# HGRN states loaded into idle split-weight buffers, prompt-state stores behind the weights, no chain offsets

## Chip, cores, metric

The kernel runs on one core of a Trainium2 chip. The metric is the device time of one execution in microseconds (us); lower is better. Of the kernel before there are three timed runs, with a median of 1349.09 us (1347.33 to 1349.79), and one profiled execution.

## What is computed

One inference step of a two-layer decoder trunk for a prompt of 256 tokens and, beside it, 8 sequences of 4 new tokens each ("sample") that carry state. All inputs are float32. For each layer:

```python
x = layer_norm(ALPHA * x + 0.5 * swiglu(x, ffn1_w_in, ffn1_w_out))
z = x @ mix_w_in                       # 1024 -> 1024 (RWKV) + 2048 (HGRN) + 512 (gMLP)
o_rw, s_rw, sh_rw = rwkv7_mix(z_rw, rw_shift0, rw_S0, ...)    # 4 heads x 64
o_hg, s_hg = hgrn2_mix(z_hg, hg_S0, lb, norm_g)               # 4 heads x 128
o_cm, v_cm = chunk_mlp_mix(z_cm, ...)
x = layer_norm(ALPHA * x + concat[o_rw, o_hg, o_cm] @ mix_w_out)
x = layer_norm(ALPHA * x + 0.5 * swiglu(x, ffn2_w_in, ffn2_w_out))
```

For the sample sequences HGRN starts from a carried state `state_hgrn` of 8 x 4 x 128 x 128 for each layer (2 MB): its output needs q times that state, and the new state is written out. For the prompt the state begins at zero. Outputs are the activations and, for each layer, the RWKV and HGRN end states of prompt and sample, the shift rows, and the normalised gMLP v rows of the sample (`cm_v_sample`).

## The kernel before

All 288 tokens lie along the free dimension, features along the partitions. Weights stream from HBM in blocks: `prep` (L338) loads one block of up to 4 x 128 rows and 256 columns (512 KB) into one of 3 buffers with the tag `raw`. For both feed-forward layers and the RWKV columns of the mixer (`rw_z`, L768) the block is then split into a high part (ScalarE, tag `wh`, 3 buffers) and a low part (VectorE, tag `wl`, 3 buffers), and each product takes three matmuls. For the HGRN and gMLP columns of `mix_w_in` (10 units of `hg_units`, L1325) and for `mix_w_out` the block is used as it is (pool "raw"), so `wh` and `wl` hold nothing between the end of `rw_z` and the first block of the second feed-forward. A `wh` or `wl` buffer is 4 KB in each partition, as is a state tile `s0` of [128, 8, 128] floats.

The mixer is written as 14 chains of small steps (`CHAINS`, L1790), generators that `mix` (L1708) walks round robin in `go`; after each step, `fill` (L435) emits one or more pieces of the ten dense units. So trace order alternates chains and dense work. A scheduler then orders each engine's instructions by priority, which is the trace position; `prio` (L83) moves the position of a chain, a step (in groups of four for a dense unit) or a chain of one layer ("@0") up by the number in `PR` (L1794), or down where it is negative. Engines run their instructions in that compiled order; a transfer issued by SyncE (SP) waits in SP's order for its buffer or its data.

The chains that matter here: `prompt` (`rw_prompt`, L952) and `post` for RWKV; `scan` (`hg_scan`, L1381), `hmix` (`hg_mix`, L1462) for the HGRN prompt; `hsam` (`hg_sample`, L1512) for the HGRN sample output, `hst` (`hg_states`, L1562) for its new states; `cm` (`cm_mix`, L1638). In `hsam`, V and K are transposed on TensorE (`hTs`, `h`) and split (`hk`); GpSimd builds masked queries `hqm`; the four states `s0` (program name `hs`) are loaded at L1544 into tiles of the tag `m4` (19 buffers shared with most mixer tiles); 64 matmuls `hp` read `hs` and `hqm`; then squares `hsqs`, a reduce and a reciprocal `hrm`, and the scaled output `hos`. `hst` updates `hs` in place and stores it (L1592). `hmix` forms `hO` for two halves of the prompt, normalises them through `hsq`, `hrm`, `hon`, transposes them back (`hot`), and stores its end state `hSP` at L1502. `rw_prompt` stores `rwSo` at L1150. `cm_mix` stores `cvn` at L1666. When the mixer outputs `x` are ready, `post` (L525) runs `mix_w_out` over them: first the k-blocks 0, 1, 6, 7 (RWKV and gMLP), then 2 to 5 (HGRN).

Of the kernel before, what the change touches and what calls it, by code (L numbers as in the profile page):

```python
# [8 lines left out]
F32 = mybir.dt.float32  # L9
# [11 lines left out]
NS = 32  # L21
# [17 lines left out]
class Trunk:  # L39
# [298 lines left out]
    def prep(self, spec):  # L338

        name, l, ks, n0, pool = spec  # L340
        nk = len(ks)
        nc = self.nc
        raw = self.wp.tile([128, 4, 256], F32, tag="raw", name=f"raw{nc.next_id()}", bufs=B["raw"])
        runs = [i for i in range(nk + 1) if i in (0, nk) or ks[i] != ks[i - 1] + 1]
        for a, b in zip(runs, runs[1:]):
            src = self.I[name][l][ks[a] * 128:(ks[b - 1] + 1) * 128, n0:n0 + 256]
            nc.sync.dma_start(raw[:, a:b], src.rearrange("(c p) n -> p c n", p=128))
        if pool == "raw":
            return raw
        hi = self.wp.tile([128, 4, 256], F32R, tag="wh", name=f"wh{nc.next_id()}", bufs=B["wh"])  # L350
        lo = self.wp.tile([128, 4, 256], F32R, tag="wl", name=f"wl{nc.next_id()}", bufs=B["wl"])
        with self.prio("prep"):
            self.act(hi[:, :nk], raw[:, :nk])
            self.sub(lo[:, :nk], raw[:, :nk], hi[:, :nk].bitcast(F32), nc.gpsimd if pool else None)
        return hi, lo
# [596 lines left out]
    def rw_prompt(self, l, KR, bh, kh, V, eP, em):  # L952

        nc, O = self.nc, self.O
# [43 lines left out]
        for qi, src in ((0, bh), (2, kh)):  # L998
# [3 lines left out]
            for h in range(2):  # L1002
                pv = ps[h].rearrange("p (j c q n) -> p j c q n", j=2, c=2, q=2)
                for k, mk in ((0, self.mst64), (1, self.min64)):
                    v = AT[qi + k].rearrange("p (j g) n -> p j g n", j=2)[:, :, 2 * h:2 * h + 2]
# [6 lines left out]
            if qi == 0:  # L1012
# [4 lines left out]
                for h in range(2):  # L1017
                    p = ps[h][:, 0:256].rearrange("p (j c n) -> p j c n", j=2, c=2)
                    v = D.rearrange("p (j g) n -> p j g n", j=2)[:, :, 2 * h:2 * h + 2]
# [8 lines left out]
        for j in range(2):  # L1028
            js = slice(j * 128, (j + 1) * 128)
            for i, src in enumerate((V, bh, kh, KR[:, :, 0])):  # L1030
                p = self.ps(f"pT{l}{j}{i}")
# [11 lines left out]
        for b in (2, 4, 8, 16, 32):  # L1043
            Ab = self.ep.tile([128, 8, 64], F32, tag="Ab", name=f"Ab{l}{b}", bufs=B["Ab"])
            self.mul(Ab, AT[0], bc(self.nmt64[b], 8), self.eng("Ab"))
            p = self.ps(f"pX{l}{b}")
            self.mm(p, self.idb, self.id8.rearrange("p g n -> p (g n)"), True, False)
            p = g8(p)
# [96 lines left out]
        p = self.ps(f"pSo{l}")  # L1145
        for c in range(2):
            self.tr(p[0:64, c * 128:(c + 1) * 128], S[:, c, 3])
        so = self.ep.tile([64, 256], F32, tag="rwSo", name=f"rwSo{l}", bufs=1)
        nc.vector.tensor_copy(so, p[0:64, 0:256])
        nc.sync.dma_start(O["rwkv_state_prompt"][l, 0].rearrange("g v k -> v g k"),  # L1150
                          so.rearrange("p (g k) -> p g k", g=4))

    def rw_load(self, l):
        nc, I = self.nc, self.I
# [307 lines left out]
    def hg_mix(self, l):  # L1462
        nc, O = self.nc, self.O
        Q, P, K, V = [self.hg(n) for n in "QPKV"]
        AT = self.hs[0]
        VT = self.m4([128, 2, 4, 128], f"hVT{l}")
        KT = self.m4([128, 2, 4, 128], f"hKT{l}")
        for i, (src, dst) in enumerate(((V, VT), (K, KT))):
            for j in range(2):
                p = self.ps(f"hT{l}{j}{i}")  # L1470
                for h in range(4):
                    self.tr(p[:, h * 128:(h + 1) * 128], self.hpr(src)[:, h, 128 * j:128 * j + 128])
                self.act(dst[:, j].rearrange("p h n -> p (h n)"), p)
                yield
        SP = self.a2(f"hSP{l}").rearrange("p c n -> p (c n)")[:, 0:512].rearrange("p (h n) -> p h n", h=4)
        on = self.m4([128, 2, 4, 128], f"hon{l}")
        self.hon = on
        for j in range(2):
            js = slice(128 * j, 128 * j + 128)
            p = self.ps(f"hO{l}{j}").rearrange("p (h n) -> p h n", h=4)  # L1480
            for h in range(4):
                self.mm(p[:, h], AT[:, 4 * j + h], VT[:, j, h], h == 0, j == 0 and h == 3)
            if j == 1:
                for h in range(4):
                    self.mm(p[:, h], self.hpr(Q)[:, h, js], SP[:, h], False, h == 3)

            sq = self.a2(f"hsq{l}{j}").rearrange("p c n -> p (c n)")[:, 0:512].rearrange("p (h n) -> p h n", h=4)
            self.act(sq, p, AF.Square)
            r = self.hrms(f"{l}{j}", sq, 4)
            self.mul(on[:, j], p, r.unsqueeze(2).to_broadcast([128, 4, 128]))  # L1490
            self.done.add(f"hm{j}{l}")
            yield
            p = self.ps(f"hS{l}{j}").rearrange("p (h n) -> p h n", h=4)
            for h in range(4):
                self.mm(p[:, h], KT[:, j, h], VT[:, j, h])
            if j == 0:
                self.act(SP, p)
            else:
                for h in range(4):
                    self.stt(SP[:, h], SP[:, h], P[:, 256 * h + 255:256 * h + 256], p[:, h], ALU.mult, ALU.add)  # L1500
            yield
        nc.sync.dma_start(O["hgrn_state_prompt"][l, 0].rearrange("h k v -> k h v"), SP)  # L1502

    def hrms(self, nm, sq, n):
        nc = self.nc
        r = self.ep.tile([128, 4], F32, tag="hrm", name=f"hrm{nm}", bufs=2)[:, 0:n]
        nc.vector.tensor_reduce(r, sq, axis=AX.X, op=ALU.add)
        self.act(r, r, AF.Sqrt, bias=self.eps[:, 2:3], scale=1.0 / 128)
        nc.vector.reciprocal(r, r)
        return r  # L1510

    def hg_sample(self, l):  # L1512
        nc, I, O = self.nc, self.I, self.O
        gp = nc.gpsimd
        SB = 4 * T
        Q, P, K, V = [self.hg(n) for n in "QPKV"]
        AS = self.hs[1]


        vs = self.ep.tile([128, 128], F32, tag="hvs", name=f"hvs{l}", bufs=1)  # L1520
        p = self.ps(f"hTs{l}")
        self.tr(p[:, 0:128], V[:, SB:])
        self.act(vs, p[:, 0:128])
        k3 = self.m4([128, 2, 4, 128], f"hk3{l}", F32R)
        for i, src in ((0, K), (1, V)):
            r3 = self.a2(f"r3{l}{i}").rearrange("p c n -> p (c n)")[:, 0:384].rearrange("p (h r t) -> p h r t", h=4, r=3)
            gp.tensor_copy(r3, self.hsm(src).unsqueeze(2).to_broadcast([128, 4, 3, 32]))
            p = self.ps(f"h3{l}{i}")
            for h in range(4):
                self.tr(p[0:96, h * 128:(h + 1) * 128], r3[:, h].rearrange("p r t -> p (r t)"))  # L1530
            pv = p.rearrange("p (h n) -> p h n", h=4)
            self.act(k3[0:96, i], pv[0:96])
            lo = slice(32, 64) if i == 0 else slice(64, 96)
            self.sub(k3[lo, i], pv[lo], k3[lo, i].bitcast(F32))
            yield

        qm = self.m4([128, 4, 8, 32], f"hqm{l}")
        for h in range(4):
            self.mul(qm[:, h], self.hsm(Q)[:, h].unsqueeze(1).to_broadcast([128, 8, 32]), self.tb, gp)
        S0 = []  # L1540
        for h in range(4):
            s0 = self.m4([128, 8, 128], f"hs0{l}{h}")
            S0.append(s0)
            nc.sync.dma_start(s0, I["state_hgrn"][l, :, h].rearrange("b k v -> k b v"))  # L1544

        p = self.ps(f"hp{l}")[:, 0:128]
        for b in range(8):
            for h in range(4):
                self.mm(p[32 * h:32 * h + 32], qm[:, h, b], S0[h][:, b], b == 0, False)
            if b % 2:  # L1550
                yield
        self.mm(p, AS, vs, False, True)
        sq = self.e(f"hsqs{l}")[:, 0:128]
        self.act(sq, p, AF.Square)
        r = self.hrms(f"{l}s", sq, 1)
        os = self.ep.tile([128, 128], F32, tag="hvs", name=f"hos{l}", bufs=1)
        self.act(os, p, scale=r)
        self.hos = os
        yield
        self.hst = S0, k3  # L1560

# [76 lines left out]
    def cm_mix(self, l, cw, m):  # L1638
# [6 lines left out]
        for j, (o, n) in enumerate(((0, 128), (128, 128), (T, NS))):  # L1645
            p = self.ps(f"cT{l}{j}")
            for c in range(2):
# [15 lines left out]
        v = vn.rearrange("p (j h) d -> p j (h d)", j=3)  # L1663
        self.mul(v, v, gb[:, 0].unsqueeze(1).to_broadcast([128, 3, 256]), gp)
        self.add(v, v, gb[:, 1].unsqueeze(1).to_broadcast([128, 3, 256]), gp)
        nc.sync.dma_start(O["cm_v_sample"][l].rearrange("b t d -> (b t) d"),  # L1666
                          vn[0:NS, 8:12].rearrange("p h d -> p (h d)"))
        yield
        M = self.a2(f"cM{l}")
        for j in range(2):  # L1670
# [37 lines left out]
    def mix(self, l, q, x, st):  # L1708
# [30 lines left out]
        def chain(name, g, *names):  # L1739

            while not all(f"{n}{l}" in self.done for n in names):
                yield False
            yield from g()
            self.done.add(f"{name}{l}")
# [15 lines left out]
        def post(f):  # L1760
# [2 lines left out]
            return f(l, q, rw["o"], *self.rwv[6:], lambda: mt(0))  # L1763

        self.rw_load(l)
        ch = {
            "pre": (pre,),
            "prompt": (lambda: self.rw_prompt(l, *rw["v"]), "pre"),
# [14 lines left out]
        m = m[0]  # L1783
        r = self.post(("mix_w_out", l), m, KC, 1.0, q["ln"][1], SHIFT[1], GROUPS[E["mo"]])
        go(*[(chain(n, *ch[n]), f, n) for n, f in CHAINS if n in LATE])
        return r


# [2 lines left out]
          ('cm', 1), ('post', 1), ('houts', 1), ('hout', 1), ('hou0', 3), ('scan', 1)]  # L1791
LATE = ()

PR = {'prep': 250, 'posts': 450, 'hou0': -50, 'scan': 400, 'hsam': -150, 'post': -400, 'scan.4': 20,  # L1794
      'cm.1': 200, 'q1.0': -7, 'hmix': 20, 'hst.6': 100, 'sample.0': -20, 'hmix.7': -20, 'posts@1': -400,
      'sample.2': 50, 'houts@0': 200, 'prompt.19': -7, 'houts': 50, 'scan@0': 400, 'houts.0': -50, 'prompt.22': 200,
      'o1': 7}

E = {'gn': 'v', 'gm': 'v', 'LN': 1, 'th': 't', 'xl': 'p', 'R1': 'p', 'mo': 'r', 'om': '', 'vb': (0, 2), 'hs': (0, 1,
     2, 3), 'Ab': 'p', 'RV': 'v', 'LL': 'v', 'S': 'p', 'P': 'p', 'KS': 'v'}  # L1800
# [43 lines left out]
```

## Time and profile before

| | before |
|---|---|
| median of 3 runs | 1349.09 us |
| the profiled execution: its own time | 1349.48 us |
| its span, first to last instruction | 1347.8 us |
| mean granted TensorE clock | 0.992 |
| TensorE matmul busy | 1315.4 us (98%) |
| VectorE, ScalarE, GpSimd busy | 65%, 44%, 16% |
| DMA, mean over the span | 144 GB/s |

Busy time is counted from the profiler's records; a matmul's end is modelled. TensorE is the engine to watch; idle time of another engine matters only where TensorE waits for it. The two mixers stand at about 250 to 465 us and 909 to 1121 us. Times in all rows are microseconds from the start of the span. "PEclk" is the granted clock as a share of full speed; "DMA share" is the mean busy share of the core's 16 DMA engines.

### The profile page before, as it was taken

How to read it: one execution, taken by the hardware profiler on the slowest of the kernel's cores; microseconds unless marked ns; L12 is line 12 of the kernel's file. 1: busy time of each engine (PE TensorE's matmuls, PEld its weight loads, DVE VectorE, ACT ScalarE, POOL GpSimd, SP SyncE). 2: the span in 40 equal slices, each digit the busy share in tenths (PEclk: the TensorE clock that was granted, in tenths of full speed). 3: DMA queues.
4: the chain of work that ended last, by engine and by line, in shares of the span. 5: the costliest groups of instructions: out<-in, count | busy, mean ns of one | idle time of the engine just before them, and what ended most of it. 6: DMA issues, size and time to landing. Idle time of an engine off the chain costs nothing.

```text
span 1347.8 us, 26357 instructions
## 1 busy us (share of the span) xinstructions
PE 1315.4 (98%) x10714; PEld 1213.6 (90%) x10714; DVE 869.9 (65%) x1670; ACT 599.2 (44%) x974; POOL 221.5 (16%) x361
## 2 busy tenths in 40 slices
PE   8999999999998999999999999999999999999998
PEld 6999999867767799999999999997777769999998
DVE  4555447865435697774698775597744359877643
ACT  5454435743143364443465444367322516544433
POOL 9200001335334100000100000022453221000002
PEclk9999999999998999999999999999999999999998
DMA  5655455431235555554555554553122455555551
GB/s 179 191 159 171 156 166 165 127 95 49 75 110 164 161 172 157 171 157 157 162 167 163 166 159 159 168 157 109 59 75 68 138 163 180 161 168 162 179 162 50
DMA packets 208151, 194.03 MB, mean 144 GB/s; under 512 B 15911, under 2 KB 206363, under 8 KB 208030
## 3 DMA queue, kind: packets, MB, share of 16 engines
q1 hardware_dynamic: 207326, 190.91, 46.0%
q8 instruction: 84, 1.38, 0.4%
q0 software_dynamic: 608, 1.31, 0.4%
q14 instruction: 37, 0.30, 0.1%
q10 hardware_dynamic: 96, 0.13, 0.0%
HBM read 185.10 MB, written 7.22 MB: 143 GB/s over the span
## 4 chain that ended last, share of the span: by engine, by line
PE 90%; DVE 5%; DMA 2%; issue 1%; ACT 1%; POOL 1%; SPq 0%; DVEq 0%; ACTq 0%
PE d L97 78%; PE hA L97 1%; DMA raw<-in_ffn_w_in 1%; PE pX L97 1%; DMA raw<-in_mix_w_out 1%; PE pE L97 1%; PE pD L97 1%; DVE ax L65 1%; PE lnd L97 1%; DVE wl L65 1%; DVE zs L77 1%; PE hp L97 0%; PE yp L97 0%; ACT wh L62 0%; PE pO L97 0%
## 5 line engine op out<-in xcount | busy, mean ns | idle before, releaser
L97 PE MATMUL d<-x,wh 128*128 128x290 f32 (+1 forms) x3072 | 623.0, 298 | 0.0
L97 PEld LDWEIGHTS d<-x,wh 128*128 128x128 f32 x3072 | 498.3, 190 | 1.5
L65 DVE TENSOR_TENSOR wl<-raw,wh 128x1024 fp32r<-128x1024 f32 (+1 forms) x288 | 346.0, 1202 | 230.2 <-ACT wh L62 229.2
L62 ACT ACTIVATE wh<-raw 128x1024 fp32r<-128x1024 f32 (+1 forms) x288 | 298.2, 1035 | 431.9 <-PE d L97 267.5
L97 PE MATMUL d<-x,wl 128*128 128x290 f32 (+1 forms) x1536 | 457.6, 298 | 2.2 <-DVE wl L65 2.2
L97 PEld LDWEIGHTS d<-x,wl 128*128 128x128 f32 x1536 | 291.2, 190 | 2.6 <-ACT x L62 2.3
L97 PE MATMUL d<-h,wh 128*128 128x288 f32 x1408 | 282.1, 296 | 0.0
L97 PEld LDWEIGHTS d<-h,wh 128*128 128x128 f32 x1408 | 226.3, 188 | 0.2
L97 PE MATMUL d<-h,wl 128*128 128x288 f32 x704 | 207.9, 295 | 0.0
L97 PE MATMUL d<-ax,raw 128*128 128x288 f32 x640 | 173.9, 414 | 0.0
L65 POOL TENSOR_TENSOR lnv<-lnq,lnq 128x288 f32<-128x288 f32 x6 | 7.6, 1273 | 840.0 <-ACT lnq L62 840.0
L97 PEld LDWEIGHTS d<-ax,raw 128*128 128x128 f32 x640 | 115.2, 190 | 30.3 <-issue 2.0
L97 PEld LDWEIGHTS d<-h,wl 128*128 128x128 f32 x704 | 132.4, 188 | 0.2
L97 PE MATMUL d<-x,raw 128*128 128x288 f32 x256 | 66.8, 409 | 2.3 <-DMA raw<-in_mix_w_out 1.6
L97 PEld LDWEIGHTS d<-x,raw 128*128 128x128 f32 x256 | 47.8, 190 | 17.0 <-DVE lns L65 1.8
L77 DVE SCALAR_TENSOR_TENSOR ax<-d,ax 128x288 f32<-128x288 f32 x48 | 21.6, 454 | 49.1 <-PE d L97 49.1
L62 ACT ACT_TABLE_LOAD x39 | 50.0, 1283 | 5.0 <-DVE yg L77 3.5
L62 ACT ACTIVATE sg<-yg,ccg 128x288 f32<-128x288 f32 x66 | 34.7, 528 | 35.3 <-DVE yg L77 35.2
L62 ACT ACTIVATE h<-sg 128x288 fp32r<-128x288 f32 x88 | 37.7, 435 | 21.7 <-DVE sg L65 20.9
L65 DVE TENSOR_TENSOR h<-sg,h 128x288 fp32r<-128x288 f32 x88 | 39.5, 454 | 5.6 <-ACT h L62 5.6
L77 DVE SCALAR_TENSOR_TENSOR yu<-nu,ccu,yu 128x288 f32<-128x288 f32 x66 | 34.0, 515 | 0.8
L77 DVE SCALAR_TENSOR_TENSOR yg<-nu,ccg,yg 128x288 f32<-128x288 f32 x66 | 33.9, 516 | 0.8
(477 smaller groups left out, 1291.1 us busy)
## 6 DMA issues: line engine op xcount, KB each, us to landing
raw<-in_ffn_w_in SPq DMA_DIRECT2D x176, 512.0 KB
raw<-in_ffn_w_out SPq DMA_DIRECT2D x80, 512.0 KB
raw<-in_mix_w_in SPq DMA_DIRECT2D x56, 512.0 KB
raw<-in_mix_w_out SPq DMA_DIRECT2D x12, 512.0 KB
raw<-in_ffn_w_out SPq DMA_DIRECT2D x16, 256.0 KB
hs<-in_state_hgrn SPq DMA_DIRECT2D x8, 512.0 KB
out_hgrn_state_sample<-hs SPq DMA_DIRECT2D x8, 512.0 KB
raw<-in_mix_w_out SPq DMA_DIRECT2D x8, 256.0 KB
```

The costliest lines, as they stand in the source:

```text
L62: self.nc.scalar.activation(out, in_, func, **kw)
L65: (eng or self.nc.vector).tensor_tensor(out, a, b, op=op)
L77: self.nc.vector.scalar_tensor_tensor(out, a, s, b, op0=op0, op1=op1)
L97: self.nc.tensor.matmul(out, lhsT, rhs, start=start, stop=stop)
```

## The change

The four HGRN state tiles of a layer are no longer `m4` tiles loaded inside `hsam`. A new function `hg_load`, called by `mix` right after `rw_load`, takes two `wh` and two `wl` buffers for them and issues the four loads on SP, behind the last weight load traced so far (`issue_after` fixes the issue order on SP and adds no wait for that load); at that place in the trace it is the last block of `rw_z`. The prompt-state stores of `rw_prompt` and `hg_mix` are collected in a list and issued at the end of `mix`, behind the last load of `mix_w_out`. The store of `cm_v_sample` goes from SP's queue to GpSimd's. All entries of `PR` but `prep` are dropped. `prep` remembers its last load.

```diff
@@ prep
-            nc.sync.dma_start(raw[:, a:b], src.rearrange("(c p) n -> p c n", p=128))
+            self.lastraw = nc.sync.dma_start(raw[:, a:b], src.rearrange("(c p) n -> p c n", p=128))
@@ rw_prompt
-        nc.sync.dma_start(O["rwkv_state_prompt"][l, 0].rearrange("g v k -> v g k"),
-                          so.rearrange("p (g k) -> p g k", g=4))
+        self.late.append((O["rwkv_state_prompt"][l, 0].rearrange("g v k -> v g k"),
+                          so.rearrange("p (g k) -> p g k", g=4)))
@@ hg_mix
-        nc.sync.dma_start(O["hgrn_state_prompt"][l, 0].rearrange("h k v -> k h v"), SP)
+        self.late.append((O["hgrn_state_prompt"][l, 0].rearrange("h k v -> k h v"), SP))
@@ new
+    def hg_load(self, l):
+
+        self.hs0 = []
+        with self.tc.issue_after(self.lastraw.ins if hasattr(self.lastraw, "ins") else self.lastraw):
+            for h in range(4):
+                s0 = self.wp.tile([128, 8, 128], F32, tag=("wh", "wl")[h % 2], name=f"hs0{l}{h}", bufs=3)
+                self.nc.sync.dma_start(s0, self.I["state_hgrn"][l, :, h].rearrange("b k v -> k b v"))
+                self.hs0.append(s0)
@@ hg_sample
-        S0 = []
-        for h in range(4):
-            s0 = self.m4([128, 8, 128], f"hs0{l}{h}")
-            S0.append(s0)
-            nc.sync.dma_start(s0, I["state_hgrn"][l, :, h].rearrange("b k v -> k b v"))
+        S0 = self.hs0
@@ cm_mix
-        nc.sync.dma_start(O["cm_v_sample"][l].rearrange("b t d -> (b t) d"),
-                          vn[0:NS, 8:12].rearrange("p h d -> p (h d)"))
+        gp.dma_start(O["cm_v_sample"][l].rearrange("b t d -> (b t) d"),
+                     vn[0:NS, 8:12].rearrange("p h d -> p (h d)"))
@@ mix
         self.rw_load(l)
+        self.hg_load(l)
+        self.late = []
...
         r = self.post(("mix_w_out", l), m, KC, 1.0, q["ln"][1], SHIFT[1], GROUPS[E["mo"]])
         go(*[(chain(n, *ch[n]), f, n) for n, f in CHAINS if n in LATE])
+
+        with self.tc.issue_after(self.lastraw.ins if hasattr(self.lastraw, "ins") else self.lastraw):
+            for dst, src in self.late:
+                self.nc.sync.dma_start(dst, src)
@@ module
-PR = {'prep': 250, 'posts': 450, 'hou0': -50, 'scan': 400, 'hsam': -150, 'post': -400, 'scan.4': 20,
-      'cm.1': 200, 'q1.0': -7, 'hmix': 20, 'hst.6': 100, 'sample.0': -20, 'hmix.7': -20, 'posts@1': -400,
-      'sample.2': 50, 'houts@0': 200, 'prompt.19': -7, 'houts': 50, 'scan@0': 400, 'houts.0': -50, 'prompt.22': 200,
-      'o1': 7}
+PR = {'prep': 250}
```

## Rows read from the trace of the kernel before

**Rows 1.** The page: busy time, share of the span and instructions of each engine.

```profile
PE 1315.4 (98%) x10714; PEld 1213.6 (90%) x10714; DVE 869.9 (65%) x1670; ACT 599.2 (44%) x974; POOL 221.5 (16%) x361
```

**Rows 2.** Windows, first mixer's tail: length, busy (count) by engine, PEclk, DMA share, GB/s.

```profile
382.50:396.60 14.10, 14.10 (x60) 11.06 (x59) 3.80 (x7) 3.38 (x6) 4.83 (x5) 1.00 0.54 153
...
402.10:408.00 5.90, 0.02 (x1) 0.05 (x2) 4.98 (x11) 3.63 (x7) 4.09 (x8) 0.72 0.94 273
408.00:412.50 4.50, 4.50 (x25) 4.10 (x26) 0.00 (x0) 1.59 (x3) 0.00 (x0) 0.60 1.03 259
...
458.80:465.30 6.50, 6.50 (x32) 5.98 (x33) 5.06 (x9) 4.16 (x8) 0.54 (x1) 0.74 0.62 194
```

**Rows 3.** Windows, second mixer's tail: busy of PE, PEld, DVE, ACT, POOL; clock; DMA.

```profile
1060.70:1069.50 8.80, 5.91 (x61) 4.32 (x60) 5.94 (x16) 7.01 (x12) 6.03 (x5) 1.00 0.93 247
...
1082.80:1085.40 2.60, 0.06 (x1) 0.07 (x2) 1.82 (x5) 1.12 (x4) 2.60 (x2) 1.00 0.56 187
```

**Rows 4.** Waits of TensorE in both tails: total us, times, longest.

```profile
PE hp L97 <- DVE hgO L77: 5.9, 1, 5.9
...
PE d L97 <- DMA raw<-in_mix_w_out: 1.4, 1, 1.4
...
PE hot L101 <- DVE hon L65: 2.5, 1, 2.5
...
PE hT L101 <- DVE hk L65: 1.5, 1, 1.5
```

**Rows 5.** Timeline of SP, both tails: start, length of the issues, what, count.

```profile
402.23 5.70 SPq L1544 DMA_DIRECT2D hs<-in_state_hgrn  x4
...
428.35 5.96 SPq L1592 DMA_DIRECT2D out_hgrn_state_sample<-hs  x4
434.40 9.91 SPq L347 DMA_DIRECT2D raw<-in_mix_w_out  x4
...
1053.97 0.46 SPq L1544 DMA_DIRECT2D hs<-in_state_hgrn  x1
1059.74 0.61 SPq L1150 DMA_DIRECT2D out_rwkv_state_prompt<-rwSo  x1
```

**Rows 6.** Timeline of VectorE and GpSimd, first tail; the bracket is idle time before.

```profile
398.59 0.86 DVE L65 TENSOR_TENSOR cM<-cbs,cO 128x256 f32<-128x256 f32 x2 [12.04 <-PE cO L97]
...
402.12 2.53 POOL L65 TENSOR_TENSOR hqm<-hgQ,tb 128x256 f32<-128x256 f32 x4
```

**Rows 7.** Timeline of VectorE, second tail.

```profile
1083.13 0.28 DVE L1507 TENSOR_REDUCE hrm1s<-hsqs 128x1 f32<-128x128 f32 x1 [8.38 <-ACT hsqs L62]
```

**Rows 8.** Windows, start of the first mixer, columns as in rows 2.

```profile
249.90:255.40 5.50, 5.50 (x43) 5.50 (x42) 5.50 (x18) 3.97 (x8) 3.08 (x10) 1.00 0.67 170
255.40:262.50 7.10, 6.66 (x34) 5.25 (x34) 6.73 (x21) 5.82 (x11) 4.13 (x14) 1.00 0.23 57
```

**Rows 9.** Timelines of SP and TensorE, start of the first mixer.

```profile
261.46 0.33 SPq L809 DMA_DIRECT2D out_rwkv_shift_prompt<-sho  x1
...
262.55 0.53 SPq L347 DMA_DIRECT2D raw<-in_mix_w_in  x1
...
266.65 6.47 PE L97 MATMUL d<-ax,raw 128*128 128x288 f32 x26
```

**Rows 10.** Chain that ended last: a weight load's landing, and the split after it.

```profile
447.83 3.63 DMA raw<-in_ffn_w_in
451.48 1.06 ACT wh L62
```

**Rows 11.** Windows, the middle of each mixer, columns as in rows 2.

```profile
300.00:382.00 82.00, 81.48 (x1230) 62.73 (x1232) 39.59 (x79) 21.98 (x46) 34.10 (x32) 1.00 0.22 66
...
959.00:1041.00 82.00, 81.94 (x1249) 63.11 (x1247) 39.46 (x78) 22.21 (x47) 34.20 (x33) 1.00 0.23 66
```

**Rows 12.** SP's wait for the gMLP rows; a GpSimd-issued transfer's time on GpSimd.

```profile
SPq L1666 <- POOL cvn L65: 3.4, 1, 3.4
...
400.21 0.53 POOL L1632 DMA_DIRECT2D cbs<-in_cm_bs  x1 [12.50 <-DVE cM L65]
```

## The prediction

> **What bounds the kernel now.** I read the page first: TensorE is busy for 98% of the span [rows 1], so a change can win only what TensorE idles or loses to a low clock: 1347.8 - 1315.4 = 32.4 us of idleness. The windows say where. The middles of both mixers are full, 81.5 and 81.9 of 82 us [rows 11]; the tails are not. In the first tail TensorE does nothing for 5.9 us, then works 4.5 us at a granted 0.60 [rows 2]; in the second it is idle for 8.80 - 5.91 = 2.9 us and later for 2.60 - 0.06 = 2.5 us [rows 3]. The waits of TensorE name the instructions: `hp`, `hT` and `hot` [rows 4].
>
> Two things stand behind these waits. **The states come late.** In the first layer SP issues the four state loads only at 402.23 [rows 5], just when TensorE has run out of work. The window moves 5.9 us x 273 GB/s = 1.6 MB and the next one 4.5 x 259 = 1.2 MB [rows 2], together what the 2.1 MB of states, one weight block of 0.5 MB and a small store need. In the second layer the first load goes at 1053.97, then SP stands at the RWKV prompt-state store until 1059.74, with three loads behind it [rows 5]. **The other engines wait for TensorE's order.** From 382.5 to 396.6 TensorE runs almost only dense matmuls of `o1`, `o0`, while VectorE, ScalarE and GpSimd are busy 3.8, 3.4 and 4.8 of 14.1 us [rows 2]; VectorE idles 12.04 us until `cO`, and `hqm` begins at 402.12, after the dense work it could have run beside [rows 6]. `hsam` carries -150, so its transposes stand behind those dense pieces.
>
> **Early state loads.** Removed from the tails: 2 x 4 loads of 512 KB and what waits for them. In the first layer I count the whole hole, 5.9 us, and the low clock after it, 4.5 x (1 - 0.60) = 1.8 us [rows 2]. In the second layer 2.9 us: three of four loads land inside that window, which moves 247 GB/s at a DMA share of 0.93 [rows 3]; 1.5 us of it is put down to `hk` [rows 4], so it could also return nothing. The 2.5 us wait of `hot` follows from the same lateness: `hrm1s`, the sample's reduce, stands on VectorE ahead of the prompt's `hrm` and waits until 1083.13 for `hsqs`, made from the last `hp` [rows 7]. With states early, `hp` ends early and this wait goes; bounds 0 and 2.5. Sum: 5.9 + 1.8 + 2.9 + 2.5 = 13.1 us.
>
> **What the loads cost where they go.** They need two `wh` and two `wl` buffers, which come free as the last RWKV blocks are consumed, some 6 us before the dense units begin at about 256. From 249.90 to 255.40 the DMA engines are 0.67 busy, from 255.40 to 262.50 only 0.23 [rows 8]: free are 5.5 x 0.33 + 7.1 x 0.77 = 7.3 us. The loads need 2.1 MB / 273 GB/s = 7.7 us. SP stands still there anyway, for the shift-row store at 261.46 [rows 9]. So I count 0, because all but 0.4 us fits; the other bound is a weight load put behind all four, below. On the far side, the second feed-forward's first split is at 451.48 [rows 10], while the state stores are issued from 428.35 and SP has gone on at 434.40 [rows 5]: the buffers are wanted 17 us after SP has passed the stores, and one of three is free throughout. Cost 0; gone if `hst` slips by more than that. Four `m4` buffers come free in the tail; that can only advance allocations there, and I count nothing.
>
> **Stores moved.** The RWKV store (0.61 us of issue) and the HGRN one no longer stand ahead of state loads and stores; the second layer's block at 1059.74 is contained in the 2.9 us. They land in SP's queue beside the first feed-forward loads, 320 KB for each layer, 1.2 us at 273 GB/s. A weight load there takes 3.63 us to land and then feeds the first split [rows 10]; bounds 0 and 1.2 us a layer. I take 0, since SP waits for a buffer before those loads. They are moved past the last `mix_w_out` loads; the 1.4 us wait for one of them [rows 4], behind the sample-state stores [rows 5], stays or goes, bounds 0 and -1.4; I leave it. The gMLP store frees SP of a 3.4 us wait and costs GpSimd about one issue, 0.53 us by its nearest row [rows 12]; nobody reads its result and GpSimd idles in that window, so 0.
>
> **Offsets dropped.** No instruction is added or removed; orders change. Removing -150 lets `hTs`, `h`, `hqm` and the splits run under the 14.1 us of dense work [rows 2], which is what the first term needs to be won. Removing +400 (+800 in the first layer) of `scan` could slow it, but the layers, with 800 and 400, and 450 and 50 for `posts`, have almost the same counts and busy times in the middle [rows 11]: offsets of this size hardly decide there. Something new will be last, though: the `hot` and `hk` waits are the nearest sizes, 2.5 and 1.5 us [rows 4], mean 2.0, and I charge one in each layer; bounds 0 and 5.9, the longest tail wait. Given back: 4.0 us.
>
> **Sum.** 13.1 - 4.0 = 9.1 us. Against the profiled execution's own 1349.48 us that is 1340.4; it stands 0.4 us above the median, so I predict 1340.0. A measurement of this kernel tells 0.2%, 2.7 us, from no change.
>
> **Rival 1: the weights wait behind the states** (slower, 0.17). If the four loads get ahead of the dense units' weight load, issued at 262.55 and used by the matmuls at 266.65 [rows 9], they delay it. A landing takes 3.6 us [rows 10], so slack is 4.1 - 3.6 = 0.5 us; a full 7.7 us ahead of it costs 7.2 us a layer, 14.4 in all, less 9.1: 1354.4 us. It decides once more than some 0.4 + 0.5 = 0.9 us of state transfers are still to come at 262.5. Against: the 7.3 free us, and buffers that come free 6 us before. For: SP's order is fixed by estimated times, and a small slip there moves four loads. The Trainium skill, "DMA: Bandwidth & Descriptors", section "Queues, rings and completion order", says that SP's transfers share one set of rings whose descriptors are consumed in order; by that rule a load queued early is no free load, and this change would come out slower wherever a weight load stands behind it. Rows 5 agree so far: three state loads stood behind one store.
>
> **Rival 2: the hole was not the states'** (no change, 0.11). The profile names `hgO` on VectorE, not a load, as what ended the 5.9 us [rows 4]. If VectorE's chain sets it, early states win nothing in the first layer (7.7 us less), and 9.1 - 7.7 = 1.4 us stays: 1348. Against: `hp` reads `hs` and `hqm`, nothing that `hgO` writes, and the transfers fill that window.
>
> **Rival 3: partly** (faster, 0.12). The first layer's hole goes, the second's waits are those of `hk` and `hon` and stay: 7.7 - 4.0 = 3.7 us, 1345.7.
>
> **Rival 4: a later chain** (slower, 0.08). Without `scan`'s offset the HGRN prompt ends after the dense work; TensorE then waits twice a layer for what is now hidden. It decides when the chain slips by more than the 14.1 us of cover [rows 2]; at 5.9 us a layer and nothing won, 1349.5 + 11.8 = 1361.
>
> **The numbers.** My forecast has 0.52. Its own range is 1332 to 1345: all 13.1 us with nothing given back, with the 1.4 us and with the low clock of 458.80 to 465.30, 6.5 x 0.26 = 1.7 us [rows 2], gives 1333; 1345 is the edge to rival 3. Faster by over 0.2%: 0.52 + 0.12 = 0.64; within: 0.11; slower: 0.17 + 0.08 = 0.25. The range runs from 1332 to 1354, up to rival 1; above it are half of that and rival 4, below it little.
>
> **What would show it.** Right: no state load on SP in either tail, state loads between about 250 and 262; `hTs` and `hqm` before the last dense pieces of `o0`; no `hp` wait over 1 us; the clock at 1.00 through the first tail; full windows at the start of the mixers. Wrong: TensorE waiting for `raw` of `mix_w_in` near 262 (rival 1), an equal hole before `hp` under another name (rival 2), or VectorE's `hon` or `hSP` as last link of a longer tail (rival 4).

## The result and the profile after

The changed kernel takes 1331.28 us, the median of 4 runs (1329.77 to 1333.56), beside 1349.44 us of the kernel before. The ratio is 0.9869, 95% interval [0.985, 0.9888]: 18.2 us or 1.3% faster. The forecast had the direction, with 9.1 us half of the size; the result is 0.7 us below the low end of the range. The profiled execution after took 1330.73 us, with a span of 1329.0 us and a granted clock of 0.998.

The page's first part after, to be held against [rows 1]:

```profile
PE 1303.8 (98%) x10714; PEld 1203.5 (91%) x10714; DVE 860.6 (65%) x1670; ACT 598.5 (45%) x974; POOL 221.4 (17%) x363
```

The same 10714 matmuls. The span fell by 18.8 us. TensorE's idle time, span less busy, went from 32.4 to 25.2 us, only 7.2 us of that; the other 11.6 us left its busy time. But for 1.8 us of low clock, that was in no step of the prediction. To find the place, each mixer's tail is cut from the last `pO` of the RWKV prompt to the end of `lnva`, the layer norm behind `mix_w_out`. The same 64 dense matmuls of the HGRN units are left over at the start of it in both kernels. First the kernel before, then the one after, windows of the two tails (columns as in rows 2):

```profile
382.55:465.32 82.77, 72.88 (x412) 58.39 (x412) 44.66 (x90) 31.82 (x70) 26.66 (x26) 0.94 0.55 161
1041.17:1121.45 80.28, 72.70 (x412) 55.84 (x412) 41.78 (x90) 31.83 (x70) 23.44 (x19) 1.00 0.53 157
```

```profile
383.29:455.33 72.04, 69.27 (x411) 54.65 (x412) 41.81 (x90) 31.73 (x70) 27.26 (x27) 1.00 0.50 151
1032.19:1104.31 72.12, 69.28 (x411) 54.64 (x412) 41.81 (x90) 31.84 (x70) 23.98 (x20) 1.00 0.48 145
```

The tails are 10.7 and 8.2 us shorter, 18.9 us in all. Idle in them fell from 9.9 and 7.6 us to 2.8 each, 11.9 us together; busy time fell by 3.6 and 3.4 us. In the second tail the granted clock was 1.00 in both kernels, so those 3.4 us are not the clock's. Outside the tails three small differences cancel: the two heads of the mixers (from `z` to the last `pO`) grew by 0.6 and 1.1 us, the feed-forward layers between the mixers stayed within 0.1 us, and the stretch from the second tail to the end of the program is 1.7 us shorter. That last one is no work of the change: its same matmuls ran at another granted level. Windows of the last 5 us with dense work, before and after:

```profile
1335.00:1340.00 5.00, 5.00 (x29) 4.67 (x28) 1.11 (x6) 2.42 (x4) 0.00 (x0) 0.66 0.01 2
```

```profile
1316.20:1321.20 5.00, 5.00 (x40) 4.68 (x40) 1.20 (x6) 2.42 (x4) 0.00 (x0) 1.00 0.00 0
```

29 matmuls against 40 in 5 us. The changed kernel itself, profiled once more, ended at 0.66 with 28 matmuls in such a window. A difference of 1 to 2 us between two profiled executions is therefore not to be read as the change's.

Waits of TensorE in the first tail after, and below the dots in the second (total us, times, longest):

```profile
PE lnd L97 <- DVE ax L77: 1.8, 1, 1.8
PE d L97 <- DMA raw<-in_mix_w_out: 0.9, 1, 0.9
...
PE lnd L97 <- DVE ax L77: 1.7, 1, 1.7
PE d L97 <- DVE lns L65: 1.1, 1, 1.1
```

Against [rows 4], `hp`, `hot` and `hT` are gone and no wait of the HGRN chains has come in their place. `lnd` is the layer norm, which waited 1.8 us before as well.

Timeline of SP after, first mixer (start, length, what, count):

```profile
250.16 3.60 SPq L1518 DMA_DIRECT2D hs<-in_state_hgrn  x3
253.79 6.66 SPq L1160 DMA_DIRECT2D sn<-in_state_rwkv  x8
...
262.63 0.58 SPq L1518 DMA_DIRECT2D hs<-in_state_hgrn  x1
263.32 0.52 SPq L347 DMA_DIRECT2D raw<-in_mix_w_in  x1
...
395.70 19.88 SPq L347 DMA_DIRECT2D raw<-in_mix_w_out  x6
419.99 5.73 SPq L1597 DMA_DIRECT2D out_hgrn_state_sample<-hs  x4
425.82 9.85 SPq L347 DMA_DIRECT2D raw<-in_mix_w_out  x4
435.72 0.61 SPq L1796 DMA_DIRECT2D out_rwkv_state_prompt<-rwSo  x1
```

Against [rows 5, 9]: the states go at 250 to 262.6, the dense units' weight load moved only from 262.55 to 263.32, and `mix_w_out` starts at 395.70 (before: 390.54).

Timeline of TensorE after, first tail:

```profile
385.81 0.60 PE L101 MATMUL hT<-ident,hgV 128*128 128x128 f32 x4
386.25 1.14 PE L97 MATMUL d<-ax,raw 128*128 128x288 f32 x4
387.31 1.09 PE L97 MATMUL cO<-cwt,cvn 128*64 128x128 f32 x16
...
393.86 0.64 PE L97 MATMUL hp<-hs,hqm 128*32 128x128 f32 x16
394.43 1.24 PE L97 MATMUL d<-ax,raw 128*128 128x288 f32 x4
...
396.92 0.60 PE L101 MATMUL pgt<-ident,OM 128*128 128x128 f32 x4
```

Where before 58 dense matmuls stood in one block, they now stand in groups of 4 to 8, with every chain's matmuls between them. Timeline of TensorE before:

```profile
382.48 14.33 PE L97 MATMUL d<-ax,raw 128*128 128x288 f32 x58
```

`cO`, on which VectorE waited 12.04 us [rows 6], is done by 389.

### The profile page after: what moved, and what is told of

It reads as the page before. It is cut to its first block, busy times and chain, and to the rows that moved or that the text cites. A ratio compares the mean times of both kernels' runs of the same rounds, so it can differ in the third digit from the quotient of the medians.

```text
span 1329.0 us, 26345 instructions
## 1 busy us (share of the span) xinstructions
PE 1303.8 (98%) x10714; PEld 1203.5 (91%) x10714; DVE 860.6 (65%) x1670; ACT 598.5 (45%) x974; POOL 221.4 (17%) x363
## 4 chain that ended last, share of the span: by engine, by line
PE 89%; DVE 4%; DMA 2%; issue 2%; ACT 1%; POOL 1%; SPq 0%; POOLq 0%; ACTq 0%; DVEq 0%
PE d L97 79%; PE hA L97 1%; DMA raw<-in_ffn_w_in 1%; PE pX L97 1%; DMA cws<-in_cm_ws 1%; PE pE L97 1%; PE pD L97 1%; DVE wl L65 1%; PE lnd L97 0%; DVE DE L65 0%; PE hO L97 0%; ACT wh L62 0%; DMA raw<-in_mix_w_out 0%; PE hp L97 0%; DVE ax L65 0%
## 5 line engine op out<-in xcount | busy, mean ns | idle before, releaser
L97 PE MATMUL d<-ax,raw 128*128 128x288 f32 x640 | 182.1, 418 | 0.0
```

The source lines that it names most:

```text
L97: self.nc.tensor.matmul(out, lhsT, rhs, start=start, stop=stop)
```

## Experiments

Each ratio is to the kernel before, timed beside it, with its 95% interval.

### One part alone

**Early states.** Kernel after with the old `PR`, both prompt-state stores and the `cvn` store as before.

```diff
-PR = {'prep': 250}
+PR = {'prep': 250, 'posts': 450, ..., 'o1': 7}
-        self.late.append(...)
+        nc.sync.dma_start(...)
```

> Only the four early state loads of each layer into the idle wh and wl buffers; the old offsets, store places and the SP store of the gMLP rows stay. Theory A (the late states made the holes; the order of the rest matters little): the 5.9 us hole before hp, the low clock after it and the 2.5 us wait of hot go, 10 to 13 us less than before, about 1338. Theory B (TensorE's order made them: hsam's -150 keeps the transposes behind 14 us of dense work, and the matmuls stay in small pieces): hp still waits for hk or hqm, 3 to 7 us less than before, about 1344, and the tails still keep TensorE busy for about 72.7 us each.

1347.95 us, 0.9985 [0.9973, 0.9998]: about 2 us. The hole is gone, yet other waits stand there. Waits of TensorE, whole span:

```profile
PE pgt L101 <- DVE OM L65: 4.1, 2, 2.1
PE d L97 <- DVE x L65: 4.1, 2, 2.8
```

So the prediction's main term, as a term of the loads, falls.

**Offsets.** Kernel before with `PR = {'prep': 250}`, nothing else.

> Only the offsets dropped (all but prep); states still loaded inside hsam into m4 tiles, stores in their old places. Theory A: the loads still come late or stand ahead of weight loads, so at most 3 us less than before, or slower by up to 5 us: 1346 to 1354. Theory B: the interleaved order alone wins 8 us or more, below 1341, with TensorE busy for about 69.3 us in each tail.

1337.55 us, 0.9908 [0.9888, 0.9929]: some 12 us, two thirds of the gain, with the loads still inside `hsam`. They now stand on SP at 392.45 instead of 402.23 [rows 5]:

```profile
392.45 5.63 SPq L1544 DMA_DIRECT2D hs<-in_state_hgrn  x4
```

**Stores.** Kernel before with the late prompt-state stores and the `cvn` store on GpSimd.

> Only the two prompt-state stores of each layer queued behind the last mix_w_out load, and the gMLP rows stored from GpSimd's queue. Both theories: the RWKV store no longer stands ahead of three state loads in the second layer, so some of its 2.9 us goes, 0 to 3 us less than before, 1346 to 1349; the first layer's 5.9 us hole stays.

1347.12 us, 0.9982 [0.997, 0.9994]: some 2 us. The state loads go at 400.86, 1.4 us earlier, and TensorE's wait now carries their name:

```profile
PE hp L97 <- DMA hs<-in_state_hgrn: 5.2, 2, 4.6
```

`hp` starts there at 405.95, before VectorE ends `hgO` at 407.19. That answers rival 2: `hp` does not wait for `hgO`, and the 5.9 us ascribed to it [rows 4] are read as a wait for the states, too. The three parts alone sum to 12.4 + 2.0 + 2.4 = 16.8 of about 17.7 us by ratios; they hardly help each other.

### One part undone

**State loads back in `hsam`**, as `m4` tiles, the rest as after.

> The changed kernel with the state loads put back inside hsam and into m4 tiles; stores late and offsets dropped. Theory A: it loses most of the gain, 1342 to 1350, with a wait of TensorE for hp of 3 us or more in one tail at least. Theory B: it keeps most, below 1337.

1336.42 us, 0.99 [0.9882, 0.9919]. Timeline of SP:

```profile
377.20 12.65 SPq L347 DMA_DIRECT2D raw<-in_mix_w_in  x3
389.94 5.15 SPq L1553 DMA_DIRECT2D hs<-in_state_hgrn  x4
```

**Idle buffers, late load.** As after, but `hg_load` is called inside `hsam`.

```diff
-        self.hg_load(l)
...
+        self.hg_load(l)
         S0 = self.hs0
```

> The changed kernel with the state tiles in the idle wh and wl buffers but traced where hsam needs them, behind the last weight load traced by then. If the early time of the loads is worth the 5.1 us that putting the loads back cost, this kernel shows that loss too, about 1336, and hp waits for hs. If the four freed m4 buffers are worth it, it stays at the changed kernel's 1331.

1331.68 us, 0.9871 [0.9854, 0.9888], the changed kernel's time with loads 130 us later. SP:

```profile
376.55 5.40 SPq L347 DMA_DIRECT2D raw<-in_mix_w_in  x2
382.00 5.12 SPq L1518 DMA_DIRECT2D hs<-in_state_hgrn  x4
388.83 0.37 SPq L347 DMA_DIRECT2D raw<-in_mix_w_in  x1
```

Earliness is not what pays. The `wh` and `wl` buffers are empty when the loads' turn comes, and they are issued at 382.00, ahead of the last `mix_w_in` block. The `m4` tiles are not: SP waits 1.6 us for ScalarE (`qs`) and 0.3 us for VectorE (`gst`) before these loads, which read only from HBM, and at 389.94 they stand behind that block. That the buffers alone set this place is not shown, since `hg_load` also brings `issue_after`. These 8 us are worth some 4 us (1336.42 against 1331.68, intervals that overlap by 0.0006).

**Fewer `m4` buffers.** As after, with 15 instead of 19, the four that the states left.

> The changed kernel with 15 m4 buffers instead of 19, so the four that the states left are taken away. If those buffers are what the state part wins (5.1 us lost with the loads put back): about 5 us slower than the changed kernel, 1336. If not: 1331, and the loss came from the loads' place in SP's queue.

1333.84 us, 0.9882 [0.9868, 0.9895]. **The kernel after once more**, beside it:

> The changed kernel itself, once more, as the yardstick of this group: 18 us less than before, a ratio of 0.987.

1332.29 us, 0.9873 [0.9859, 0.9886]. The 1.5 us between them lie within the intervals: the four freed buffers have no effect that could be told. **Stores as before**, the rest as after:

> The changed kernel with the three stores back in their old places and queues. The RWKV store has no state load behind it any more; if nothing else waits for SP there: no change, 1331. If mix_w_out's loads wait behind them: 1 to 2 us slower, as the two runs with states in hsam differ (1337.6 without, 1336.4 with the late stores).

1333.18 us, 0.9876 [0.9862, 0.9889]: nothing to tell either. The 2 us that the stores won alone are not found again once the loads don't stand behind them.

### Which offset

**Before without `hsam`'s -150:**

> The kernel before with one entry of PR taken out, hsam -150; all else as before. Theory B1 (this one entry keeps the sample chain behind the dense pieces): 8 us or more less than before, near the 12.9 us of dropping all offsets, below 1342. Theory B2 (several entries together, post -400 and the rest too): under 4 us less, 1346 or more.

1345.22 us, 0.9965 [0.9953, 0.9978]: 4 to 5 us, and TensorE now waits 6.2 us for `x` (line below). **Before without `hsam`, `post` and `posts@1`:**

> The kernel before with three entries of PR taken out, hsam -150, post -400 and posts@1 -400. If post's offset is the second half of the matter (without hsam's the matmuls of mix_w_out waited 6.2 us in all for x, which post and posts write): a further 5 us or more below the run without hsam alone, 1340 or less, and those waits under 2 us. If the rest is spread over the other entries: 1343 to 1346.

1337.38 us, 0.9913 [0.9893, 0.9932]: these three entries are nearly all of the 12 us, and the waits for `x` are gone. **After with `'post': -400` put back:**

> The changed kernel with one entry put back, post -400. If that entry delays the RWKV output: waits of mix_w_out's matmuls for x of 3 us or more in all, 3 to 8 us slower than the changed kernel, 1334 to 1339. If not: 1331.

1342.02 us, 0.9949 [0.9934, 0.9964], 0.76% or 10 us lost to one entry. TensorE's longest wait there, and the same line without `hsam`'s entry in the kernel before:

```profile
PE d L97 <- DVE x L65: 6.2, 4, 1.8
```

`post` in `PR` is the chain that writes RWKV's part of the mixer output `x` on VectorE, not the function of the same name that runs `mix_w_out`. With -400 it falls behind: in the first tail it writes `x` at 411.8 and 412.6, without it at 398.3 and 398.7. TensorE comes to the `mix_w_out` matmuls that read it before it is written; these waits are 6.2 of the 10 us, and the rest was not traced. **After with `'hsam': -150` put back:**

> The changed kernel with one entry put back, hsam -150. Theory B1: it loses 8 us or more, to 1339 or more, and hp starts after the last dense piece of o0 again. Theory B2: it loses less than 4 us, below 1335.

1346.46 us, 0.9976 [0.9967, 0.9986]: this entry alone takes back some 14 of the 18 us. So -150 and -400 each cost 10 to 14 us alone, and some 12 together in the kernel before (with `posts@1`): taking only one of them out could show little. Timeline of TensorE, first tail:

```profile
383.85 14.82 PE L97 MATMUL d<-ax,raw 128*128 128x288 f32 x60
398.50 0.27 PE L101 MATMUL hTs<-ident,hgV 128*128 128x128 f32 x1
...
398.72 0.60 PE L101 MATMUL hT<-ident,hgV 128*128 128x128 f32 x4
399.25 1.09 PE L97 MATMUL cO<-cwt,cvn 128*64 128x128 f32 x16
...
405.73 0.41 PE L97 MATMUL hp<-hs,hqm 128*32 128x128 f32 x2 [2.31 <-POOL hqm L65]
```

The block of dense matmuls is back, with `hTs` behind it. Not only `hsam` is late: `hT` of the HGRN prompt and `cO` of gMLP carry no offset and are 13 and 12 us later than after.

### Why one offset holds the other chains

**A PSUM tile of its own.** The kernel after with -150 for `hsam`, and with `hTs`, `h` and `hp` in one tile of their own and three instead of four tiles for the rest.

```diff
-        return self.pm.tile([128, 512], F32, tag="m", name=name)
+        return self.pm.tile([128, 512], F32, tag="m", name=name, bufs=3)
-        p = self.ps(f"hTs{l}")
+        p = self.pm.tile([128, 512], F32, tag="n", name=f"hTs{l}", bufs=1)
...
```

> The changed kernel with hsam -150 put back (as in the run that lost nearly all), but hTs, h and hp of hsam in a PSUM bank of their own, so three banks are left for the other chains. Theory C (the chains share four PSUM banks that are handed out in trace order, so the late hTs holds back hT, cO and pgt of the other chains): hT, cO and pSo run between the last dense pieces again while hTs stays behind them; 4 to 10 us less than that run, 1336 to 1342. Theory D (the offset acts through hsam alone, whose own chain is the last link): no gain, 1345 or more.

The order came back: only `hsam`, from `hTs` on, is late.

```profile
386.13 0.60 PE L101 MATMUL hT<-ident,hgV 128*128 128x128 f32 x4
387.64 1.09 PE L97 MATMUL cO<-cwt,cvn 128*64 128x128 f32 x16
...
402.05 0.27 PE L101 MATMUL hTs<-ident,hgV 128*128 128x128 f32 x1
```

So it is the shared PSUM tiles, handed out in trace order, that hold the others behind `hsam`. The time did not come back: 1351.2 us, 1.0016 [1.0002, 1.003], and `hot` waits for `hon` 2.6 us in each layer, as it does with the shared tiles.

**The same tiles without -150:**

> The changed kernel, with the sample's transposes (hTs, the three h pieces) and its hp in a PSUM tile of their own and three tiles instead of four for the rest, but without hsam's -150. Theory P (the three tiles cost nothing by themselves; with -150 the sample's own late chain is what costs): 1331 to 1336 us, ratio 0.987 to 0.990, and the separate tile with -150 therefore loses its 15 us or so to the chain alone. Theory Q (three tiles for the rest are too few, and that, not the offset, is what made the separate tile with -150 slow): 1342 us or more, ratio 0.995 or more, with waits for pgt and d under the names of other chains.

1336.18 us, 0.9902 [0.9885, 0.9918]. Fewer tiles for the rest cost some 4 us (0.9902 against 0.9873 and 0.9869). With the separate tile -150 costs 1.0016 - 0.9902 = 1.14%, 15 us; with shared tiles 0.9976 - 0.9873, 14 us. So the tied order is not what costs. What is left as the price is the sample's own chain, started 14 us late; that it ends last is read from the wait for `hon`, which [rows 7] tie to the sample's squares on VectorE, and was not tried by itself. These waits are 5.2 of the 15 us; where the rest goes stays open.

### Beyond the change

**Loads after `pre`.** `hg_load` is called once the RWKV inputs are made.

> The changed kernel with the four state loads traced after the chain pre, so behind a weight load of the first dense units, where the DMA engines moved 39 GB/s from 286 to 300 us. If the waits of cwp for cws at the start of the mixers (2.1 us in all) and the lengthening of the heads (0.6 and 1.1 us) come from the state loads beside that transfer, they go: 1 to 2 us less than the changed kernel, about 1329.5. If the order of the heads makes them, no change: 1331.

1329.92 us, 0.9861 [0.9845, 0.9878]. The loads go at 272.88, and a wait that the change brought into the heads is gone. Waits of TensorE in the heads of the kernel after, first and second:

```profile
PE cwp L101 <- DMA cws<-in_cm_ws: 0.8, 1, 0.8
...
PE cwp L101 <- DMA cws<-in_cm_ws: 1.3, 1, 1.3
```

**Sample-state stores on GpSimd's queue**, on top of that.

```diff
-            nc.sync.dma_start(O["hgrn_state_sample"][l, :, h].rearrange("b k v -> k b v"), s0)
+            gp.dma_start(O["hgrn_state_sample"][l, :, h].rearrange("b k v -> k b v"), s0)
```

> An attempt at less time than the changed kernel: the states loaded after pre, and the four new-state stores issued from GpSimd instead of SP, so that the mix_w_out loads no longer stand behind stores that wait for VectorE. If SP's order makes the waits for raw of mix_w_out (3.4 us in all in the run that loads after pre): they go, 1 to 3 us less, about 1328. If the bandwidth does (2 MB of stores beside the loads, DMA share near 1): no change, 1330.

1326.8 us, 0.984 [0.9823, 0.9856], and timed again, beside the repeated kernel after:

> States loaded after pre and new states stored from GpSimd, once more beside the changed kernel: if the 1326.8 us of its first run stand, 3 to 5 us less than the changed kernel, ratio 0.984, intervals apart.

1328.65 us, 0.9839 [0.9823, 0.9855], against 0.9873 [0.9859, 0.9886]. This version beats both kernels, the changed one by 3.6 us. What the stores give of that was not timed beside the loads after `pre` alone (0.9861 and 0.984, intervals that overlap). Its SP issues the ten `mix_w_out` loads without a store between them:

```profile
394.26 38.95 SPq L347 DMA_DIRECT2D raw<-in_mix_w_out  x10
```

In its first profile the waits for `raw` of `mix_w_out`, 3.4 us with the loads after `pre` alone, are gone, and `lnd` alone, 1.8 and 1.9 us, is left in the tails.

## Why the prediction was right in direction and wrong in size

**What bounds the kernel: held.** The gain lies in the two tails, 18.9 us, and the middles gave nothing.

**Early state loads, 13.1 us: the waits went, for another reason.** `hp`, `hT` and `hot` are gone as forecast, but the loads alone brought 2 us. Early states without the new order leave `pgt` and `d` waiting; the new order without early states brings 12. The step took the full DMA share and the states as cause, where the chains' late place in TensorE's order was the larger one: it set when `hqm` and its followers began, and, by holding `hsam`'s tiles, when the loads stood on SP. Worth some 4 us beside the new offsets, the loads owe that to their place ahead of a weight block on SP, not to being 130 us early.

**"Offsets dropped", counted only as "what the first term needs": the step that failed.** It is the largest term of the change, 12 of 18 us. Two things were not read. The waits of `d` for `x` that `post` -400 makes hardly showed in the kernel before (0.5 us in the first tail), where `hsam` was later still; they come out as soon as `hsam` is freed (6.2 us). And the test for "offsets of this size hardly decide" was made on `scan` in the middles [rows 11], where dense work covers everything; the tails have no cover.

**Given back, 4.0 us: nothing.** No chain is late in either tail after. The nearest rows were waits of the old order, and that order went. Of the 9.1 us by which the sum was short, these are 4.0.

**Not in the sum: 7.0 us of busy time in the tails**, less 1.8 us foreseen as low clock in the first. Of the first tail's 3.6 us another 1.7 are the low clock of 458.80 to 465.30 [rows 2], which the prediction kept for the end of its range; the granted clock of that tail is now 1.00. In the second, at a clock of 1.00 in both, 3.4 us remain: see the last section.

By kind: idle was forecast at 5.9 + 5.4 - 4.0 = 7.3 us and came to 11.9; busy time at 1.8 and came to 7.0. 9.8 us more than foreseen, of which the heads took back 1.7, and the end of the program gave the 1.7 that are the clock's.

**Loads at the head, 0: 1.7 us.** Three went where it was said, the fourth at 262.63, behind the shift-row stores. Rival 1 is out for the large price: the weight load moved 0.8 us and its matmuls didn't wait. But the small `cws` load, not looked at, lands 5.5 and 6.1 us after its issue, against 4.0 and 3.3 before, and TensorE waits 0.8 and 1.3 us for it; with the loads after `pre` it lands in 3.9 and 3.4 us. GpSimd issues it, at 256.39, so it does not stand behind the states in SP's queue; it shares the DMA engines with them, whose busy share from 255.40 to 262.50 went from 0.23 [rows 8] to 0.96. The Trainium skill, "DMA: Bandwidth & Descriptors", section "Queues, rings and completion order", has descriptors of one ring consumed in the order in which they are queued; this wait is no case of it, and no run here shows its price. Nor do [rows 5]: SP waits 5.3 us for `rwSo` before it issues that store, and the three loads are not yet issued.

**Stores, 0: held** beside the rest (0.9876 against 0.9873). The `mix_w_out` wait, left at 1.4, is 0.9 us after.

**Rivals.** 2 (the hole not the states'): the run with the stores alone has `hp` start before `hgO` ends, and with early states the hole is gone. 3 (the second layer keeps its waits): its tail won 8.2 us. 4 (a later chain): no such wait came.

## What to carry to other kernels

An order tuned by hand belongs to the loads and buffers that it was tuned with: when those change, cost each offset as an edit of its own, and look for its price in the stages without cover. A chain that is placed late can cost its own length at the end of the stage, and through shared buffers it takes along chains that carry no offset, here at no price that could be told. Ask of a load first whether its buffer is empty when its turn comes, and keep stores that wait for a compute engine off the queue that brings the weights.

## What had not been expected

**`hp` matmuls in pairs between dense ones cost TensorE time that no row of PE shows as idle.** Timeline of TensorE before, second tail; the time is read from start to start:

```profile
1078.25 0.41 PE L97 MATMUL hp<-hs,hqm 128*32 128x128 f32 x2
1078.59 0.75 PE L97 MATMUL d<-x,raw 128*128 128x288 f32 x2
1079.27 0.41 PE L97 MATMUL hp<-hs,hqm 128*32 128x128 f32 x2
```

Two `hp` take 0.34 us and the two dense ones behind them 0.68. After, sixteen `hp` take 394.43 - 393.86 = 0.57 us, and eight dense ones 2.04, second tail:

```profile
1040.72 2.11 PE L97 MATMUL d<-ax,raw 128*128 128x288 f32 x8
1042.76 0.65 PE L97 MATMUL hp<-hs,hqm 128*32 128x128 f32 x16
```

That is 0.17 us for an `hp` in a pair and 0.036 in a sixteen, 0.34 for a dense one in a pair and 0.255 in an eight. The three pairs from 1078.25 to 1081.31 took 3.06 us; at the prices of the long groups they would take 6 x 0.036 + 6 x 0.255 = 1.75. In the second tail `hp` as a whole was busy 4.95 us before and 2.97 after for the same 66 matmuls:

```profile
1041.17:1121.45 80.28, 4.95 (x66) 2.71 (x66) 0.63 (x2) 1.00 0.53 157
```

```profile
1032.19:1104.31 72.12, 2.97 (x66) 1.81 (x66) 0.64 (x2) 1.00 0.48 145
```

Short groups as such are not what costs. In the same tail single transposes stand between pairs of dense matmuls:

```profile
1055.27 0.27 PE L101 MATMUL hTs<-ident,hgV 128*128 128x128 f32 x1
1055.38 0.65 PE L97 MATMUL d<-ax,raw 128*128 128x288 f32 x2
1055.87 0.27 PE L101 MATMUL h<-ident,r 128*96 128x128 f32 x1
```

The transpose takes 0.11 us and the pair behind it 0.49, or 0.245 for each. `hp` differs in form: its weights have 32 columns (128*32), those of the transposes and dense matmuls shown 96 or 128. The weights of `hTs` are loaded from 1055.03, 0.24 us ahead of it; those of an `hp` pair and of the dense pair behind it only from 1078.25 and 1078.59, with their matmuls. By these rows it is the change between `hp` and the others that costs, and longer groups need fewer changes. That this is the cause of all 3.4 us was not tried by itself; these rows account for `hp` and the pairs beside it.
